# One decoder step on one core: output-projection products in attention's last iterations, weight factors by quarters, more PSUM banks for two output projections

## The chip, the cores and the metric

The kernel runs on one core of one Trainium2 chip. The core has five engines that run side by side, each with its own queue of instructions: TensorE (PE in the rows) multiplies, VectorE (DVE), ScalarE (ACT) and GpSimd (POOL) work on elements, and SyncE (SP) issues most of the transfers between the chip's main memory (HBM) and the on-chip memory (SBUF). TensorE's results go to PSUM, which has eight banks of 128 x 512 float32. The metric is the device time of one execution in microseconds; the kernel before took 2910.5 us, the median of three runs (2903.79 to 2911.71).

## The reference, cut to what matters

One step of a two-layer decoder, for a prompt of 2048 positions and for eight sequences with four new positions each (32 rows, "the sample"). Layer 0 is a gated linear attention, layer 1 an attention over a window of 128 positions and the position itself:

```python
def gla_mixer(h, state0, norm_g, w_in, w_gate2, b_gate, out_norm_g, w_out):
    u = rmsnorm(h, norm_g)
    proj = u @ w_in                       # q, k, v, gate, low-rank gate
    ...
    o, state = gla_recurrence(q, k, v, log_a, state0)
    o = rmsnorm(o, out_norm_g).reshape(bsz, seq_len, BRANCH_WIDTH).astype(h.dtype)
    return (o * jax.nn.silu(gate)) @ w_out, state

def swa_out(o, gate, w_out):
    bsz, seq_len = o.shape[:2]
    return (o.reshape(bsz, seq_len, BRANCH_WIDTH) * jax.nn.silu(gate)) @ w_out

        if layer < N_A_LAYERS:
            ...
            hp, hs = hp + dp, hs + ds
            k_p, v_p = shared_kv(hp, kv_norm, w_k, w_v, k_norm, pos_p)
        else:
            q_p, g_p = swa_query(hp, b_norm[j], b_w_in[j], b_q_norm[j], pos_p)
            hp = hp + swa_out(swa_banded(q_p, k_p, v_p, b_sinks[j]), g_p, b_w_out[j])
            q_s, g_s = swa_query(hs, b_norm[j], b_w_in[j], b_q_norm[j], pos_s)
            hs = hs + swa_out(attend(q_s, k_s, v_s, pos_s, kpos_s, b_sinks[j]), g_s, b_w_out[j])
```

The model width is 1024, the branch width 2048; layer 1 has 32 heads of 64 in 4 groups that share keys and values.

## The kernel before

The prompt is cut into 16 chunks of 128 positions. Each factor of a large product is held as two half-precision parts, high and low, and a product is three passes (high times high, high times low, low times high).

Layer 0 goes through 4 heads x 4 blocks of 4 chunks (h, j). Beside its work stand "preparation steps": they load layer 1's weights, combine and split them on VectorE, GpSimd and ScalarE, and write them to HBM (`wfd`, 7 factors wf0 to wf6) or keep them. `PR` says how many of them (`some(PR[j])`) are woven into each chunk of the block j; what remains is dealt out to the output projection of layer 0, seven to each of its chunks.

Layer 0's output projection (`a_out`, lines 1049 to 1080) takes one chunk after another, each in two halves of 512 columns with 48 products each. `load` fetches the four operands of a chunk with transposing DMAs (tiles sg or v) one chunk ahead, `fin` fetches the input (tile X), adds it to the product on VectorE (line 1064, tiles E and st), stores the sum to `hd`, and normalises the chunk after its second half. Both halves put their product in one of two PSUM banks named pj.

Layer 1's attention (from line 1661) runs 67 iterations. Iteration n projects chunk n % 16 of the group n // 16 (queries, gates, and keys and values in group 0), takes the scores of the chunk two iterations back, and the values of the chunk three back. These three lists are merged by the string ORDER: f is a piece of the projection (the "fill"), A one of four pairs of score heads, B one of two value steps. TensorE's instructions are held in exactly this order (`pin`, line 91). A value step (products kv <- rmask,sth and kv <- rmask,pst of the trace, where rmask holds V) needs the probabilities transposed, which two DMAs on SP's queue do (tiles sth and pst, line 1279); a score pair goes over VectorE (row maxima, line 1268), ScalarE (exponential) and both (split, tile v, line 198) to that queue. At the end of an iteration one step of the sample's attention (`boundary`) is taken: 9 steps of norms and caches, and twice the three steps att (scores, tile ssm), att_2 (transposes and values) and att_3 (product with the gate).

The last three iterations (n = 64, 65, 66) have no chunk left to project. They are filled with products of layer 1's output projection. That one takes 2 chunks at a time (a "pair") and does a 2 x 2 block product with 7 products instead of 8 (`Pair`, PRODS): each is 24 matrix products (0, 1 and 6 on raw operands; 2 to 5 on sums of operands). `load` fetches raw operands with transposing DMAs from `ogd2` (oge in the trace), `sums` forms the others on VectorE and ScalarE (lines 1569 to 1595, among the tiles Sh, wraw, X, ogT, qe, ke), and `fin` adds a finished product to the result (line 1601). The weight factors come from wfd, four DMAs each, all four in one go (`wform`, `wform_big`, tiles W and uT). Six products of pair 0 fill the three iterations; after them the pairs follow one another, each woven with the loads and the sums of the next. The sample's own projection (`out_sample`, with `sproj_steps`) runs in two halves after the pairs 3 and 5, on the banks pj.

Of the kernel before, what the change touches and what calls it, by code (L numbers as in the profile page):

```python
# [56 lines left out]
PR = (2, 4, 2, 0)  # L57
# [17 lines left out]
def _body(tc, nc, cp, sb, ps, dr, i, o):  # L75
# [555 lines left out]
    def sproj_steps(tiles, nk, act_hi_lo, kts=None):  # L631
# [4 lines left out]
        def one(x, w):  # L636
            if x % 8 == 0:
                n = min(8, len(tiles) - x)
                box.append(PT("pj", [P, 512], bufs=2)[:, : n * 2 * SMP].rearrange("p (x z t) -> p x z t", z=2, t=SMP))
# [410 lines left out]
    def a_out(c):  # L1050
# [28 lines left out]
        for half, w in enumerate((wo, wo1)):  # L1079
            st, box = proj_steps(lambda: PT("pj", [P, 512], bufs=2), lambda k, a: ot[k // 8 * 2 + a][:, k % 8, :], w, 16)  # L1080
            out.append(st + [lambda half=half, box=box: fin(half, box[0])])
        return load, out

    def out_sample(tiles, half, finish_s, kts=None, sc=OSC):
        st, total = sproj_steps(tiles, len(kts or range(16)), lambda: ogTs[0], kts)
# [435 lines left out]
    def wform_big(n, parts=1):  # L1521
        t = T("uT", [P, 8, 2, 512], F16, 4)
        for x in range(parts):
            ks = slice(x * 8 // parts, (x + 1) * 8 // parts)
            nc.sync.dma_start(t[:, ks], wfd[n][:, ks])
        wf[n] = lambda k, hl, s=ALL: t[:, k, hl, s]

    def wform(n):
        ts = []
        for x in range(4):  # L1530
            t = T("W", [P, 2, 2, 512], F16, NW)
            nc.sync.dma_start(t, wfd[n][:, 2 * x : 2 * x + 2])
            ts.append(t)
        wf[n] = lambda k, hl, s=ALL: ts[k // 2][:, k % 2, hl, s]
# [4 lines left out]
    TEMP = ("wraw", "Sh", "wraw", "Sh", "wraw", "bt", "bt", "og")  # L1539
# [7 lines left out]
    class Pair:  # L1547
# [3 lines left out]
        def load(self, x):  # L1551

            first = (("og", "lvm"), ("qT", "kT"), ("bt", "bt"), ("S", "sg"))[x]
            ts = [T(tag, [P, 8, P], F16, BUFS.get(tag, 2)) if self.p == 0 else ring("raw", RAW, [P, 8, P], F16) for tag in first]
            for hl in range(2):
                nc.sync.dma_start(ts[hl], ogd2[2 * self.p + x // 2][:, hl, x % 2], transpose=True)
            self.r[x] = ts
            if x != 2:
                self.l[{0: 0, 1: 1, 3: 6}[x]] = ts

        def sums(self):
# [4 lines left out]
            def whole(x, z):  # L1566
                t = ring("temp", TEMP, [P, 512], F32)
# [4 lines left out]
            def put(n, z, t):  # L1572
                if z == 0:
                    self.l[n] = [ring("form", FORM, [P, 8, P], F16) for _ in range(2)]
# [21 lines left out]

            return [lambda f=f, z=z: f(z) for f in (one, two, three, four) for z in range(2)]
# [220 lines left out]
```

## Time and profile before

| what | value |
|---|---|
| median of 3 runs | 2910.5 us (2903.79 to 2911.71) |
| the profiled execution | 2902.2 us |
| its span in the profile | 2900.4 us |
| TensorE busy | 2740.0 us, 94% |
| VectorE busy | 1854.8 us, 64% |
| ScalarE busy | 1440.1 us, 50% |
| GpSimd busy | 1059.9 us, 37% |

The span is what the profile covers from the first to the last instruction; the execution's own time is 1.8 us more. The engines overlap, so the shares do not add up to 100%. The profile also gives the granted clock of TensorE, 1.00 being 2.4 GHz and 0.50 being 1.2 GHz, and DMA's share, the mean busy share of 16 DMA engines (it can exceed 1.00 in a short stretch, since transfers overlap). A timeline row reads: start, duration, engine, line, operation, result <- operands, count, and in brackets the idle time before it and what ended it. In rows of TensorE the line is that of a helper (L101), and tiles tell the place. Tile names are reused: X is a query operand in attention, a formed operand in a pair and an input in a_out.

### The profile page before, as it was taken

How to read it: one execution, taken by the hardware profiler on the slowest of the kernel's cores; microseconds unless marked ns; L12 is line 12 of the kernel's file. 1: busy time of each engine (PE TensorE's matmuls, PEld its weight loads, DVE VectorE, ACT ScalarE, POOL GpSimd, SP SyncE). 2: the span in 40 equal slices, each digit the busy share in tenths (PEclk: the TensorE clock that was granted, in tenths of full speed). 3: DMA queues.
4: the chain of work that ended last, by engine and by line, in shares of the span. 5: the costliest groups of instructions: out<-in, count | busy, mean ns of one | idle time of the engine just before them, and what ended most of it. 6: DMA issues, size and time to landing. Idle time of an engine off the chain costs nothing.

```text
span 2900.4 us, 51645 instructions
## 1 busy us (share of the span) xinstructions
PE 2740.0 (94%) x19070; PEld 1385.9 (48%) x19070; DVE 1854.8 (64%) x3815; ACT 1440.1 (50%) x3385; POOL 1059.9 (37%) x1463
## 2 busy tenths in 40 slices
PE   6899999999999999997999999999999999978999
PEld 4445444444454444444444555555555555534444
DVE  5766787677768775346213665677767767756553
ACT  6655655465546554434212555566666666631110
POOL 2241233222322221136104676666566557520000
PEclk9999999999999999998999999999999999989999
DMA  8351334124312533799765565867867788887542
GB/s 212 85 123 44 88 120 149 38 80 151 118 37 89 169 100 95 175 234 284 180 161 145 109 128 118 201 116 131 174 112 133 164 157 159 159 194 161 108 103 70
DMA packets 765782, 389.68 MB, mean 134 GB/s; under 512 B 620752, under 2 KB 690328, under 8 KB 765496
## 3 DMA queue, kind: packets, MB, share of 16 engines
q1 hardware_dynamic: 752568, 350.65, 53.8%
q0 software_dynamic: 10880, 35.66, 3.4%
q8 instruction: 149, 2.44, 0.4%
q14 instruction: 105, 0.86, 0.1%
q10 hardware_dynamic: 2080, 0.07, 0.0%
HBM read 138.90 MB, written 107.54 MB: 85 GB/s over the span
## 4 chain that ended last, share of the span: by engine, by line
PE 38%; DVE 8%; DMA 7%; ACT 6%; issue 4%; POOL 4%; SPq 1%; DVEq 0%; POOLq 0%; ACTq 0%
PE pj L101 24%; PE tr L101 8%; PE o L101 4%; ACT o L1273 2%; PE kv L101 2%; ACT v L197 1%; DVE v L198 1%; DVE o L1268 1%; DMA pst<-v 1%; DMA sg<-oge 1%; DMA sth<-v 1%; DVE lev L1268 1%; DMA X<-qe 1%; DMA kT<-in_b_w_out_dram 1%; ACT lev L1273 1%
## 5 line engine op out<-in xcount | busy, mean ns | idle before, releaser
L101 PE MATMUL pj<-W,uT 128*128 128x512 f16 x5064 | 1193.2, 381 | 8.4 <-DVE sg L478 2.6
L101 PEld LDWEIGHTS <-uT 128*128 128x128 f16 x6880 | 643.0, 98 | 713.9 <-issue 44.5
L101 PE MATMUL tr<-W,uT 128*128 128x512 f16 x1536 | 365.5, 379 | 0.0
L186 POOL TENSOR_SCALAR rs_m<-ss 128x1 f32<-128x1 f32 (+3 forms) x190 | 45.2, 238 | 738.2 <-ACT og L611 255.7
L101 PEld LDWEIGHTS <-X 128*128 128x128 f16 x2752 | 185.2, 98 | 169.6 <-issue 30.2
L1273 ACT ACTIVATE o<-o,mx 128x256 f32<-128x256 f32 (+1 forms) x384 | 168.6, 439 | 177.9 <-DVE mx L1268 170.2
L101 PE MATMUL pj<-uT,W 128*128 128x512 f16 (+1 forms) x912 | 188.3, 357 | 26.9 <-DMA uT<-ogT 24.2
L1268 DVE CUSTOM_DVE_ANT_0 o<-o,madd,nsink 128x256 f32<-128x256 f32 (+1 forms) x384 | 184.1, 479 | 42.0 <-PE o L101 37.0
L198 DVE SCALAR_TENSOR_TENSOR v<-o,v 128x512 f16<-128x512 f32 (+1 forms) x192 | 129.0, 672 | 111.4 <-ACT v L197 94.9
L187 POOL TENSOR_TENSOR rs_r<-rs_m,mhalf 128x1 f32<-128x1 f32 (+2 forms) x186 | 185.1, 995 | 14.4
L101 PEld LDWEIGHTS <-W 128*128 128x128 f16 x2448 | 130.1, 99 | 113.7 <-issue 19.4
L101 PE MATMUL pj<-W,v 128*128 128x512 f16 x736 | 177.6, 382 | 3.8 <-DVE E L1064 3.8
L101 PEld LDWEIGHTS <-v 128*128 128x128 f16 x1008 | 98.5, 99 | 130.1 <-issue 16.4
L101 PE MATMUL pj<-W,sg 128*128 128x512 f16 x592 | 146.6, 381 | 1.2 <-DVE E L1064 1.2
L195 POOL TENSOR_TENSOR ogT<-og,ogT 128x512 f16<-128x512 f32 x68 | 88.2, 1297 | 158.0 <-ACT ogT L194 153.5
L508 POOL TENSOR_TENSOR E<-bt 128x256 f32<-128x256 f32 x96 | 71.1, 741 | 195.5 <-DVE X L195 112.2
L101 PEld LDWEIGHTS <-sth 128*128 128x128 f16 x2080 | 109.8, 98 | 51.1 <-DMA sth<-v 9.7
L101 PE MATMUL o<-gl,X 128*128 128x256 f16 (+1 forms) x768 | 113.2, 270 | 15.9 <-DMA X<-qe 6.9
L101 PEld LDWEIGHTS <-sg 128*128 128x128 f16 x800 | 78.2, 98 | 97.9 <-issue 6.8
L1273 ACT ACTIVATE lev<-lev,mx 128x256 f32<-128x256 f32 (+1 forms) x128 | 56.5, 442 | 121.2 <-DVE mx L1268 119.1
L197 ACT ACTIVATE v<-o 128x512 f16<-128x512 f32 (+1 forms) x192 | 111.2, 579 | 6.9 <-DMA sth<-v 3.3
L101 PE MATMUL kv<-rmask,sth 128*128 128x64 f16 x1984 | 104.7, 193 | 7.3 <-DMA sth<-v 7.3
(444 smaller groups left out, 5008.6 us busy)
## 6 DMA issues: line engine op xcount, KB each, us to landing
pre<-pst POOLq DMA_DIRECT2D x72, 256.0 KB, 3.5
W<-pre SPq DMA_DIRECT2D x36, 512.0 KB
ogd<-ogT SPq DMA_DIRECT2D x68, 256.0 KB
wraw<-in_a_w_in_dram SPq DMA_DIRECT2D x64, 256.0 KB
wraw<-in_b_w_in_dram SPq DMA_DIRECT2D x64, 256.0 KB
oge<-ogT SPq DMA_DIRECT2D x64, 256.0 KB
wraw<-in_a_w_out_dram SPq DMA_DIRECT2D x32, 256.0 KB
X<-in_x_prompt_dram SPq DMA_DIRECT2D x32, 256.0 KB
```

The costliest lines, as they stand in the source:

```text
L101: return order(nc.tensor.matmul(*a, **k))
L186: pool.tensor_scalar(m[:n, :k], ss, a, b, ALU.mult, ALU.add)
L187: pool.tensor_tensor(r[:n, :k], m[:n, :k], mhalf[:n, :k], ALU.pow)
L195: eng.tensor_tensor(lo, src, hi, ALU.subtract)
L197: act(hi, src, AF.Copy, scale=sc)
L198: dve.scalar_tensor_tensor(lo, src, sc, hi, ALU.mult, ALU.subtract)
L508: pool.tensor_tensor(Ev[:, :, 0, :], ref, btv[:, :, 0, :], ALU.subtract)
L1268: dve.tensor_tensor_reduce(pm[:, z], pm[:, z], madd.rearrange("p a b -> p (a b)")[:, (2 - nk) * P :], -0.125, nsink[:, g * GRP + h : g * G ...
L1273: act(pm[:, z], pm[:, z], AF.Exp, scale=-1.0, bias=nm_[:, h : h + 1], accum_out=bx["sum"][:, h : h + 1])
```

## The change

- Layer 0: `PR` goes from (2, 4, 2, 0) to (1, 4, 2, 0), so nine of its 72 preparation steps there are left to the output projection.
- Layer 0's output projection: half 1 of each chunk takes one of two banks o instead of one of two banks pj.
- The sample's output projections of both layers: half 0 takes the bank lev, half 1 the bank kv, instead of pj.
- Last three attention iterations: they hold products 0 and 1 of pair 0; products 0 and 1 of pair 1; half 0 of the sample's output and product 2 of pair 0. The operands of these products 0 and 1 are fetched at the end of iteration 56 into one tile uT. Pair 0's sums are made in the iterations 65 and 66, one step after another; its other raw operands are loaded in iteration 64 (a list `trickle`, one entry at each third f).
- Weight factors are fetched one quarter per call; those of the last iterations go through `trickle` too.
- The sample's attention steps of the last group are taken twice in each iteration from n = 52 on (at the seventh f, and at the end).
- The tile names of the sums change, and the next pair's loads and sums are woven in another order; half 1 of the sample's output stays after pair 5.

```diff
...
-PR = (2, 4, 2, 0)
+PR = (1, 4, 2, 0)
...
-    def sproj_steps(tiles, nk, act_hi_lo, kts=None):
+    def sproj_steps(tiles, nk, act_hi_lo, kts=None, bank=("pj", 2)):
...
-                box.append(PT("pj", [P, 512], bufs=2)[:, : n * 2 * SMP].rearrange("p (x z t) -> p x z t", z=2, t=SMP))
+                box.append(PT(bank[0], [P, 512], bufs=bank[1])[:, : n * 2 * SMP].rearrange("p (x z t) -> p x z t", z=2, t=SMP))
...
-            st, box = proj_steps(lambda: PT("pj", [P, 512], bufs=2), lambda k, a: ot[k // 8 * 2 + a][:, k % 8, :], w, 16)
+            st, box = proj_steps(lambda half=half: PT(("pj", "o")[half], [P, 512], bufs=2), lambda k, a: ot[k // 8 * 2 + a][:, k % 8, :], w, 16)
...
-        st, total = sproj_steps(tiles, len(kts or range(16)), lambda: ogTs[0], kts)
+        st, total = sproj_steps(tiles, len(kts or range(16)), lambda: ogTs[0], kts, (("lev", "kv")[half], 1))
...
+    def wform_big(n, x, box={}):
+        if x == 0:
+            t = box[n] = T("uT", [P, 8, 2, 512], F16, 4)
+            wf[n] = lambda k, hl, s=ALL: t[:, k, hl, s]
+        ks = slice(2 * x, 2 * x + 2)
+        nc.sync.dma_start(box[n][:, ks], wfd[n][:, ks])
+    def wform(n, x, ts={}):
+        t = ts[n, x] = T("W", [P, 2, 2, 512], F16, NW)
+        nc.sync.dma_start(t, wfd[n][:, 2 * x : 2 * x + 2])
+        wf[n] = lambda k, hl, s=ALL: ts[n, k // 2][:, k % 2, hl, s]
+    quarters = lambda f, n: [lambda x=x: f(n, x) for x in range(4)]
...
         def load(self, x):
-            first = (("og", "lvm"), ("qT", "kT"), ("bt", "bt"), ("S", "sg"))[x]
+            first = (("og", "lvm"), ("qT", "kT"), ("bt", "bt"), ("S", "qe"))[x]
             ts = [T(tag, [P, 8, P], F16, BUFS.get(tag, 2)) if self.p == 0 else ring("raw", RAW, [P, 8, P], F16) for tag in first]
+            self.fetch(x, ts)
+            self.r[x] = ts
+            if x != 2:
+                self.l.setdefault({0: 0, 1: 1, 3: 6}[x], ts)
+        def fetch(self, x, ts):
             for hl in range(2):
                 nc.sync.dma_start(ts[hl], ogd2[2 * self.p + x // 2][:, hl, x % 2], transpose=True)
-            self.r[x] = ts
-            if x != 2:
-                self.l[{0: 0, 1: 1, 3: 6}[x]] = ts
...
+                if self.p == 0:
+                    tag = ("E", "wraw", "wraw", "wraw")[x]
+                    t = T(tag, [P, 512], F32, BUFS.get(tag, 2))
+                else:
+                    t = ring("temp", TEMP, [P, 512], F32)
...
-                    self.l[n] = [ring("form", FORM, [P, 8, P], F16) for _ in range(2)]
+                    own = {2: ("ke", "ke"), 3: ("qe", "X"), 4: ("X", "st"), 5: ("sg", "sg")}[n]
+                    self.l[n] = [T(tag, [P, 8, P], F16, BUFS.get(tag, 2)) if self.p == 0 else ring("form", FORM, [P, 8, P], F16) for tag in own]
...
+            if self.p == 0:
+                return [lambda f=f, z=z: f(z) for z in range(2) for f in (one, two, three, four)]
             return [lambda f=f, z=z: f(z) for f in (one, two, three, four) for z in range(2)]
...
+    trickle, summing = [], []
+    def s_out(half):
+        cols = [slice(z * P, (z + 1) * P) for z in range(4)]
+        right = [k + 2 for k in UP]
+        fs, kts = ((0, 2, 5), UP + UP + right) if half else ((0, 3), UP + right)
+        return out_sample([lambda k, hl, z=z: wf[fs[k // 8]](k % 8, hl, z) for z in cols], half, b_finish_s, kts, OSCB)
...
-            x = 2 * (n - TOT)
-            fill = pairs[0].steps(x) + pairs[0].steps(x + 1)
+            fill = (pairs[0].steps(0) + pairs[0].steps(1), pairs[1].steps(0) + pairs[1].steps(1), s_out(0) + pairs[0].steps(2))[n - TOT]
...
                 upto = len(fill) * seen // nf
                 run(fill[done:upto])
                 done = upto
+                if trickle and seen % 3 == 0:
+                    trickle.pop(0)()
+                if boundary and seen == 7 and n > TOT - NCH + 3:
+                    boundary.pop(0)()
+                if summing and seen % 6 == 3:
+                    summing.pop(0)()
             elif lists[x]:
                 lists[x].pop(0)()
...
-        if n in (TOT - 8, TOT - 5, TOT - 3):
-            wform_big((0, 2, 1)[(TOT - 8, TOT - 5, TOT - 3).index(n)], 4)
+        if n == TOT - 8:
+            t_ = T("uT", [P, 8, 8, P], F16, 4)
+            for x in range(4):
+                pr = pairs[x // 2]
+                pr.l[x % 2] = [t_[:, 2 * x], t_[:, 2 * x + 1]]
+                pr.fetch(x % 2, pr.l[x % 2])
+        if n in (TOT - 6, TOT - 3):
+            run(quarters(wform_big, {TOT - 6: 0, TOT - 3: 2}[n]))
         if n == TOT - 4:
-            wform(3)
-        if n == TOT - 2:
-            pairs[0].load(0)
+            run(quarters(wform, 3))
         if n == TOT - 1:
-            for x in (1, 3, 2):
-                pairs[0].load(x)
+            trickle += [lambda x=x: pairs[0].load(x) for x in (3, 2, 0, 1)] + quarters(wform_big, 1)
         if n == TOT:
-            wform_big(4, 4)
-            run(pairs[0].sums())
+            trickle += quarters(wform, 4) + quarters(wform, 5)
+            summing += pairs[0].sums()
         if n == TOT + 1:
-            wform(5)
-            pairs[1].load(0)
-            pairs[1].load(1)
-        if n == TOT + 2:
-            wform(6)
-            pairs[1].load(3)
-            pairs[1].load(2)
+            trickle += quarters(wform_big, 6)
         if boundary:
             boundary.pop(0)()
...
+    run(trickle + summing)
     for p_ in range(NCH // 2):
         more = []
         if p_ + 1 < NCH // 2:
             nxt = pairs[p_ + 1]
-            if p_ > 0:
-                more += [lambda x=x, nxt=nxt: nxt.load(x) for x in (0, 1, 3, 2)]
-            more += nxt.sums()
-        weave([f for n in range(0 if p_ else 6, 7) for f in pairs[p_].steps(n)], more)
-        if p_ in (3, 5):
-            cols = [slice(z * P, (z + 1) * P) for z in range(4)]
-            right = [k + 2 for k in UP]
-            fs, kts = ((0, 3), UP + right) if p_ == 3 else ((0, 2, 5), UP + UP + right)
-            run(out_sample([lambda k, hl, z=z, fs=fs: wf[fs[k // 8]](k % 8, hl, z) for z in cols], p_ // 5, b_finish_s, kts, OSCB))
+            ld, sm = [lambda x=x, nxt=nxt: nxt.load(x) for x in (2, 3, 0, 1)], nxt.sums()
+            more = ld[:2] + sm[:2] + ld[2:3] + sm[2:6]
+        weave([f for n in range((3, 2, 0)[min(p_, 2)], 7) for f in pairs[p_].steps(n)], more)
+        if more:
+            run(ld[3:] + sm[6:])
+        if p_ == 5:
+            run(s_out(1))
```

The first place is TensorE in the second of the last three iterations, around the last pair of scores (o <- gl,X; gl holds keys). Before:

```order
L101 LDWEIGHTS sg_30681
L101 MATMUL pj_31410<-W_31329,sg_30681 128x512
L101 LDWEIGHTS X_30667
L101 MATMUL o_30997<-gl_15589,X_30667 128x256
L101 LDWEIGHTS X_30930
L101 MATMUL o_31008<-uT_29803,X_30930 128x512
L101 LDWEIGHTS ogT_30931
L101 MATMUL o_31008<-uT_29803,ogT_30931 128x512
```

And in the changed kernel:

```order
L101 LDWEIGHTS uT_29222
L101 MATMUL pj_30920<-W_30209,uT_29222 128x512
L101 LDWEIGHTS X_30805
L101 MATMUL o_31018<-gl_15563,X_30805 128x256
L101 MATMUL pj_31029<-uT_29734,uT_29222 128x512
```

After the scores stood a product 2 of pair 0 on formed operands (X, ogT); now stands a product on the early tile uT, with no sum before it.

The second place is SP's queue from the iteration 63 on (line 1279 transposes probabilities; line 1556, now 1563, loads raw operands of a pair; lines 1525 and 1532 fetch weight factors). Before:

```order
L1532 DMA W_31325<-wf_135 128x2048
L1532 DMA W_31327<-wf_135 128x2048
L1525 DMA uT_30920<-wf_133 128x2048
L1556 DMA_TRANSPOSE qT_30676<-oge_113 128x8x128
L1279 DMA_TRANSPOSE sth_30624<-v_30594 128x8x128
L1279 DMA_TRANSPOSE pst_30626<-v_30595 128x8x128
L629 DMA oge_125<-ogT_30656 512x1x256
L1230 DMA_TRANSPOSE X_30667<-qe_30664 128x8x128
L1556 DMA_TRANSPOSE kT_30677<-oge_113 128x8x128
L1556 DMA_TRANSPOSE S_30680<-oge_114 128x8x128
L1556 DMA_TRANSPOSE sg_30681<-oge_114 128x8x128
```

And in the changed kernel:

```order
L1532 DMA W_31161<-wf_134 128x2048
L1532 DMA W_31216<-wf_134 128x2048
L1527 DMA uT_30925<-wf_130 128x2048 x2
L1563 DMA_TRANSPOSE bt_30847<-oge_114 128x8x128
L1279 DMA_TRANSPOSE sth_30762<-v_30732 128x8x128
L1279 DMA_TRANSPOSE pst_30764<-v_30733 128x8x128
L629 DMA oge_125<-ogT_30794 512x1x256
L1230 DMA_TRANSPOSE X_30805<-qe_30802 128x8x128
L1563 DMA_TRANSPOSE S_30834<-oge_114 128x8x128
L1563 DMA_TRANSPOSE qe_30835<-oge_114 128x8x128
L1563 DMA_TRANSPOSE qT_30916<-oge_113 128x8x128
L1279 DMA_TRANSPOSE sth_30906<-v_30816 128x8x128
```

The loads of qT and kT, which stood around the second pair of transposes, are now behind bt, S and qe, which pair 0's sums need first; one more weight fetch stands ahead.

The third place is VectorE at the first sums of pair 0 (line 1569, now 1577). Before:

```order
L1609 TENSOR_TENSOR E_30914<-E_30914,st_30829 128x512
L198 SCALAR_TENSOR_TENSOR v_30744<-o_30810,v_30743 128x512
L1569 TENSOR_TENSOR Sh_30927<-bt_30684,bt_30685 128x512
L1268 ISA lev_30842,mx_30741<-lev_30842,madd,nsink 128x256
L1268 ISA mx_30741 128x1
L1268 ISA o_30861,mx_30741<-o_30861,madd,nsink 128x256
L198 SCALAR_TENSOR_TENSOR v_30841<-lev_30842,v_30840 128x512
L1315 SCALAR_TENSOR_TENSOR wraw_30900<-kv_30781,sg_30233 128x512
L1569 TENSOR_TENSOR wraw_30925<-S_30680,sg_30681 128x512
```

And in the changed kernel:

```order
L198 SCALAR_TENSOR_TENSOR v_30932<-o_30953,v_30931 128x512
L1612 SCALAR_TENSOR_TENSOR st_31010<-pj_30920,E_31007 128x512
L1268 ISA o_31018,mx_31014<-o_31018,madd,nsink 128x256
L1268 ISA mx_31014 128x1
L1577 TENSOR_TENSOR wraw_31036<-S_30834,qe_30835 128x512
L1577 TENSOR_TENSOR wraw_31038<-bt_30846,bt_30847 128x512
L1589 TENSOR_TENSOR wraw_31036<-wraw_31036,wraw_31038 128x512
L1594 TENSOR_TENSOR wraw_31038<-E_31098,wraw_31038 128x512
L1595 TENSOR_TENSOR E_31098<-wraw_31036,E_31098 128x512
L195 TENSOR_TENSOR ke_31042<-wraw_31036,ke_31041 128x512
L198 SCALAR_TENSOR_TENSOR v_31017<-o_31018,v_31016 128x512
```

The first sum stood behind the first eviction of pair 0, alone and ahead of two score pairs; now two sums stand between two row maxima of the last score pair, and the formed operands follow at once.

## Rows read from the trace of the kernel before

**Rows 1.** The page: its first line, part 1 (busy time, share and instructions of each engine), and one link of the chain of waits (start, length, engine, tile, line, count).

```profile
span 2900.4 us, 51645 instructions
...
PE 2740.0 (94%) x19070; PEld 1385.9 (48%) x19070; DVE 1854.8 (64%) x3815; ACT 1440.1 (50%) x3385; POOL 1059.9 (37%) x1463
...
2677.09 10.36 PE tr L101 x48
```

**Rows 2.** Windows over the last three attention iterations and the pairs behind them. Columns: stretch, its length, then busy time (instructions) of PE, PEld, DVE, ACT and POOL, the granted clock, DMA's share, GB/s.

```profile
2544.20:2616.20 72.00, 53.59 (x361) 26.01 (x361) 39.87 (x90) 22.86 (x66) 10.74 (x17) 0.88 0.84 182
2616.20:2632.20 16.00, 8.91 (x91) 3.94 (x87) 13.81 (x23) 5.18 (x9) 1.16 (x1) 0.68 1.16 237
2632.20:2735.00 102.80, 101.50 (x507) 46.52 (x505) 67.09 (x110) 16.10 (x28) 0.00 (x0) 1.00 0.55 116
2735.00:2750.00 15.00, 9.33 (x117) 5.16 (x114) 4.77 (x8) 0.28 (x1) 0.00 (x0) 0.77 0.57 144
2750.00:2896.50 146.50, 146.43 (x851) 69.37 (x848) 70.11 (x113) 16.69 (x29) 0.00 (x0) 1.00 0.38 88
```

**Rows 3.** The timeline of TensorE in the same stretches: those of its rows before which it stood idle.

```profile
2549.46 0.23 PE L101 MATMUL kv<-rmask,sth 128*128 128x64 f16 x2 [1.24 <-DMA sth<-v]
...
2550.37 0.20 PE L101 MATMUL kv<-rmask,pst 128*128 128x64 f16 x1 [0.67 <-DMA pst<-v]
...
2556.37 1.03 PE L101 MATMUL pj<-W,qT 128*128 128x512 f16 x2 [3.02 <-DMA qT<-oge]
...
2563.07 0.61 PE L101 MATMUL pj<-W,kT 128*128 128x512 f16 x1 [5.67 <-DMA kT<-oge]
...
2580.83 0.39 PE L101 MATMUL o<-uT,ogT 128*128 128x512 f16 x1 [2.19 <-DVE ogT L195]
...
2588.96 0.60 PE L101 MATMUL o<-gl,X 128*128 128x256 f16 x4 [3.37 <-DVE v L198]
...
2625.78 1.04 PE L101 MATMUL o<-uT,X 128*128 128x512 f16 x2 [6.38 <-ACT X L194]
...
2743.22 1.01 PE L101 MATMUL pj<-uT,v 128*128 128x512 f16 x2 [5.67 <-DVE st L1601]
```

**Rows 4.** Windows over five short stretches after such stops, the last one in layer 0's output projection. Columns as in rows 2.

```profile
2556.00:2566.20 10.20, 4.16 (x11) 1.47 (x12) 0.38 (x1) 0.00 (x0) 0.00 (x0) 0.50 1.13 184
2590.00:2597.00 7.00, 5.69 (x17) 2.07 (x16) 3.26 (x10) 2.65 (x7) 0.00 (x0) 0.51 0.34 65
2620.80:2631.00 10.20, 4.51 (x11) 1.40 (x12) 9.14 (x18) 3.92 (x7) 0.00 (x0) 0.50 1.26 247
2740.30:2747.00 6.70, 3.78 (x9) 1.28 (x9) 1.38 (x2) 0.00 (x0) 0.00 (x0) 0.50 0.89 214
1361.30:1375.00 13.70, 8.20 (x137) 6.47 (x137) 8.74 (x10) 6.50 (x13) 9.19 (x13) 0.50 1.09 244
```

**Rows 5.** The waits of TensorE: what it wanted to write, for whom it waited, total us, times, longest us.

```profile
PE kv L101 <- ACT v L197: 9.7, 4, 3.2
PE pj L101 <- DVE st L1064: 9.0, 2, 8.0
...
PE o L101 <- DVE mxs L1462: 5.6, 5, 2.1
...
PE pj L101 <- DVE E L1064: 5.0, 2, 3.8
...
PE tr L104 <- DVE ssg L657: 2.4, 1, 2.4
```

**Rows 6.** The timeline of SP's queue at the start of the last three iterations (start, us, line, operation, result <- source).

```profile
2539.80 4.44 SPq L1279 DMA_TRANSPOSE sth<-v  x1
2544.34 4.01 SPq L1279 DMA_TRANSPOSE pst<-v  x1
...
2552.06 3.13 SPq L1279 DMA_TRANSPOSE sth<-v  x1
2555.28 1.26 SPq L1279 DMA_TRANSPOSE pst<-v  x1
```

**Rows 7.** The timeline of TensorE, VectorE and GpSimd in the last group, at one attention step of the sample (o <- Sh,sq its scores, ssm its weights, tr <- idf,ssm their transposes, ogT the product written), with a value step and a score pair of the prompt between.

```profile
2327.34 0.31 PE L101 MATMUL o<-Sh,sq 128*32 128x128 f16 x8
...
2330.72 0.30 DVE L1468 TENSOR_SCALAR ssm<-ssm,mxs 128x160 f32<-128x160 f32 x1
...
2332.17 0.22 PE L101 MATMUL kv<-rmask,sth 128*128 128x64 f16 x2
...
2332.87 0.59 PE L101 MATMUL pj<-W,uT 128*128 128x512 f16 x2
2333.30 0.60 PE L101 MATMUL o<-gl,X 128*128 128x256 f16 x4
2333.74 1.46 PE L101 MATMUL pj<-W,uT 128*128 128x512 f16 x6
...
2341.78 0.38 PE L104 MATMUL tr<-idf,ssm 128*128 128x128 f32 x2
...
2345.27 0.80 POOL L195 TENSOR_TENSOR ogT<-spp,ogT 128x128 f16<-128x128 f32 x2
```

**Rows 8.** The timeline of VectorE at the first sum of pair 0.

```profile
2567.94 0.69 DVE L1569 TENSOR_TENSOR Sh<-bt,bt 128x512 f32<-128x512 f16 x1 [11.56 <-DMA bt<-oge]
2568.55 0.49 DVE L1268 CUSTOM_DVE_ANT_0 lev<-lev,madd,nsink 128x256 f32<-128x256 f32 x1
```

## What I predicted before the run

> **What bounds the kernel now.** Start with the page [rows 1]: TensorE works 94% of the span, VectorE 64%, and the long links of the chain of waits are bundles of 48 products of 10.36 us, so 0.2158 us for one 128x512 product. The number of products is the same in both kernels, so the time can only move through what is left besides them: TensorE's idle time, and stretches where its granted clock is half. The window view looks for both in the place that the change rewrites, from the last three attention iterations to the end [rows 2]. There TensorE is idle 18.41 + 7.09 + 1.30 + 5.67 + 0.07 = 32.5 us of 352.3, and nearly all of that lies before 2632 and in 2735 to 2750. The timeline of those stretches names each stop [rows 3]: probabilities' transposes (1.24 + 0.67), the operands qT and kT of pair 0's first product (3.02 + 5.67), formed operands (2.19, 6.38), a softmax weight v (3.37), and the bank pj (5.67). In three of four of these stretches the windows show the granted clock at 0.50, the 1.2 GHz level, and in the fourth at 0.51 [rows 4]: TensorE had stood idle just before, and it was busy 5.69 + 4.16 + 4.51 + 3.78 = 18.1 us at that level, which at the full level would be 9.1 us less. So 41.6 us stand in this part to be won. A second place is layer 0's output projection: 5.0 + 9.0 us of waits for VectorE's eviction of line 1064, 2.4 us for the sample's tile ssg [rows 5], and half clock afterwards, 8.2 us busy, 4.1 us too long [rows 4]. That is 20.5 us.
>
> **The tail, part by part.** *Operands of the first products.* qT and kT are loaded before on SP's queue behind transposes that run slowly: 4.44 and 4.01 us where the next pair has 3.13 and 1.26 [rows 6]. The change loads the raw operands of the first products of pairs 0 and 1 eight iterations before, into one tile. The 3.02 and 5.67 go, and products that need no sums fill the second iteration, so the 2.19 and 6.38 for formed operands go too; the sums of pair 0 get two iterations instead of one. *What is late next.* SP keeps its order, and the value transposes (sth, pst) still stand behind weight fetches, nine at that place against eight. I keep the 1.9 us of rows 3 for the first pair. For the others I count: pst of the second pair ends on SP at 2555.28 + 1.26 = 2556.5, and TensorE starts 2.0 us after such an end (2550.37 less 2544.34 + 4.01) [rows 3, 6], so at 2558.5. Between two value steps of an iteration stand 24 products and three scores of 0.44 us (2333.74 less 2333.30), 6.5 us; from 2551.1, where the first pair is done with its 0.7 us (2332.17 to 2332.87) [rows 7], TensorE would be there at 2557.6: 0.9 us late. The chunk after it comes behind X, S, qe and qT: four of 1.3 us from 2557.3, two of 1.3 us, and 2.0 us, together 2567.1. TensorE asks for it after 0.7 us of values, 24 products and a score, 2564.8: 2.3 us late. The bank lev, on which the sample's output waits until the last scores are read, and VectorE's second half of the sums I put at 3 us, pairs 1 and 2, whose sums come sooner after their loads, at 2 us; an estimate between nothing and the 3.37 of v [rows 3], nearer to that. One stretch at half clock stays, 2 us as in 2556 to 2566 [rows 4]. That leaves 12 of 41.6: **30 us won** (at best 41.6, at worst about 12, the case below). *The sample's output.* Its two halves no longer take a pj bank, so product 0 of the pair after it doesn't wait for the eviction of line 1601: the 5.67 and half of the 3.78 are in that sum. *Weight fetches in quarters.* As many bytes, spread between products; DMA's share there is 0.84 to 1.16 [rows 2], so they neither vanish nor grow. I put the wait of SP for the last write of oge before the early load at 1 us, between 0 and the 5.67 that one late operand costs.
>
> **Layer 0's output projection.** Half 1 goes to the banks "o", so four evictions may be outstanding and not two. Of the 20.5 us gross that would take the waits and the half clock behind them. But VectorE's eviction itself waits: the input tile X for it, and the tiles E and st that the store must have left, come from SP's queue, and the transposes of chunk c+2 are queued there behind the store of chunk c. DMA's share is 1.09 in the window at 1361 to 1375 [rows 4], so what doesn't wait for a bank may wait for an operand. I take **half, 10 us**; the bounds are -20 and +3 (one more stop of about the size of the 2.4 [rows 5]).
>
> **The last group's sample steps.** They run twice per iteration there and end seven iterations sooner. Of the chain of one attention step, scores to normalised weights take 2327.34 to 2331.02, 3.7 us, and from the transposes at 2341.78 to the written product at 2346.07, 4.3 us [rows 7]. Two of these steps now have about 16 products, 3.5 us, between them, and TensorE's order is pinned, so the shortfall of 0.2 and 0.8 us, and the sharing of the bank kv two products after, fall on TensorE in part of some fifteen steps. I take **+3 - 1.5** (an iteration that ended with two sample norms loses one), between 0 and +8, 15 times half a microsecond.
>
> **Weight preparation.** Nine of 72 steps move from layer 0 to the output projection, one each into the first block of a row; their DMAs and POOL work go with them. TensorE waits 9.7 us in four places for v in layer 0 and next to it [rows 5]; one step less can shorten these, and the stage that receives them has a DMA share over 1. **-1**, between -9.7 (all of these waits) and +5 (the whole of the E wait doubled).
>
> **The sum.** -30 + 1 - 10 + 1.5 - 1 = -38.5, rounded to -37 because the pieces of the tail overlap. The profiled execution took 2902.2 us, so 2865; the median of the runs shown, 2910.5, is 8.3 above it, so **2873 us**.
>
> **Rivals.** *The queue heads keep the loss.* Before, VectorE stood 11.56 us in front of the first sum, waiting for the load bt, with the row maxima of the next scores behind it [rows 8]. The change puts sums of pair 0 between scores again: their loads S, qe and bt stand on SP among transposes that took 4 us in a bad moment [rows 6]. If VectorE stops there once more as long, 11.6 us come back, with the 3.4 of v behind it [rows 3] and 3 of half clock: 18, and the total is -19, 2891. For it speaks that the loads' place moved by an iteration only; against it that the sums are taken one by one after 12 to 18 products and z by z. The Trainium skill ("TensorE: Matmul & The Clock Gate", section on the array's architectural detail) says that ScalarE's and VectorE's queues are strictly first in, first out, while TensorE's may pull weight loads ahead; the trace agrees, since the row maximum behind the sum started 0.6 us after it and not in the 11.56 us before [rows 8]. By that rule alone, a late bt costs its whole lateness, and the sum would be -37 + 11.6 = -25, 2885. *The banks don't bind.* Then the waits of line 1064 only change their name to X, sg or v loads, and the moved steps cost 3: -37 + 10 + 3 = -24, 2886. *The doubled sample steps stop the pinned order.* If each of the fifteen waits for its whole chain, because its input is written by POOL or ScalarE behind the prompt's work, it costs up to the 3.5 us that lay between: 15 x 3.5 = 52, and the total is +15, **2926**. It decides from 37 / 15 = 2.5 us a step on; before, the stops for mxs were 2.1 us at the longest [rows 5].
>
> **How the numbers follow.** The forecast has 0.62, the queue heads 0.20, the banks 0.10, the sample steps 0.08. 0.3% of the median is 8.7 us, about what a measurement of this kernel tells from no change. The forecast and most of the second and third case lie under 2901.8: 0.62 + 0.14 + 0.09 = 0.85 faster; the rest of these two, 0.07, is within; 0.08 slower. The range: below, -38 in the tail, -14 in the projection and -4 in layer 0 give 2910.5 - 56 = 2854; above, the second case with the sample steps at +8 and the projection at nothing gives 2891 + 6.5 + 4 (part of the ten), about 2902.
>
> **What would show it.** Right: no stop for qT or kT, and windows with the clock near 1.0 from 2550 to 2640; no stop of 5.67 before product 0 after a sample output; the rows for st and E of line 1064 gone, with less than 10 us of new waits for loads; small stops for sth and pst at the start of the tail. Wrong: a VectorE row of a sum with some 10 us of idle before it (second case); waits of pj or o for X, sg or v in the projection, as long as those that went (third); rows of ssm, skn, mxs or ogTs that wait 2 us and more, many times, in the last group (fourth). The forecast falls if TensorE's busy time at full clock grows, which none of the edits should do.

## The result, and the profile after

The changed kernel takes 2880.05 us in the median of four runs (2877.55 to 2887.28), the kernel before on the same chip 2910.97 (2903.79 to 2911.71): a ratio of 0.9903, interval 0.9879 to 0.9928, or 28 us (21 to 35) less. The forecast was 2873 us, 37 less, with a range of 2854 to 2902: the time lies in the range. The gain is three quarters of the forecast, and the forecast 37 lies just outside the interval of 21 to 35. The profiled executions are 2902.2 and 2877.55 us, 24.7 apart. The runs of the kernel before that accompany the experiments spread from 2895.7 to 2915.9, so one profile alone does not tell a few microseconds.

First the page of the changed kernel, to be read beside [rows 1]:

```profile
span 2875.8 us, 51606 instructions
...
PE 2735.2 (95%) x19070; PEld 1386.7 (48%) x19070; DVE 1850.9 (64%) x3815; ACT 1441.6 (50%) x3385; POOL 1062.2 (37%) x1463
```

As many products as before. Where did the time go? Four stages answer: layer 0 up to the second half of its first output chunk; then its output projection and, behind it, the first iterations of attention; attention from there up to iteration 64; and the rest, the tail. The windows of the kernel before (columns as in [rows 2]):

```profile
0.00:1175.59 1175.59, 1101.05 (x6966) 531.45 (x6967) 842.52 (x1516) 678.44 (x1266) 306.48 (x465) 0.98 0.38 107
1175.59:1652.88 477.29, 458.82 (x2635) 217.37 (x2634) 189.79 (x336) 152.14 (x353) 164.36 (x239) 0.98 0.78 185
1652.88:2544.61 891.73, 860.83 (x7568) 486.47 (x7567) 626.14 (x1622) 548.82 (x1637) 577.53 (x745) 1.00 0.73 147
2544.61:2896.43 351.82, 319.34 (x1906) 150.63 (x1903) 195.62 (x342) 60.70 (x132) 11.49 (x16) 0.95 0.57 124
```

And of the changed kernel:

```profile
0.00:1164.22 1164.22, 1099.55 (x6967) 531.65 (x6968) 835.39 (x1507) 672.99 (x1257) 301.82 (x456) 0.98 0.37 104
1164.22:1642.65 478.43, 454.78 (x2636) 215.83 (x2635) 193.65 (x345) 158.88 (x362) 171.40 (x248) 0.98 0.80 195
1642.65:2541.77 899.12, 867.15 (x7628) 489.36 (x7627) 627.83 (x1633) 550.29 (x1642) 576.86 (x745) 0.99 0.73 145
2541.77:2871.77 330.00, 313.77 (x1846) 149.89 (x1843) 193.31 (x332) 59.39 (x127) 12.15 (x16) 0.98 0.64 141
```

The differences of the second column are -11.4, +1.1, +7.4 and -21.8. The forecast had -1, -10, +1.5 and -29, together -38.5; these two profiles have -24.7. Two of the terms are ten off, in opposite directions. The products of the last two stages also have to be read with care: 60 of them, of the sample's last attention step, moved from the tail (x1906, now x1846) to the stage before it (x7568, now x7628). They are small, some 3 us of TensorE's time together, which belong to neither the gain of the one nor the loss of the other.

**Layer 0.** Its idle time, length less busy time, went from 74.5 to 64.7 us. TensorE's waits for v, 9.7 us in [rows 5], are 5.3:

```profile
PE kv L101 <- ACT v L197: 5.3, 4, 1.9
```

**The tail.** The idle time went from 32.5 to 16.2 us. The stops that are left, in TensorE's timeline of the changed kernel (to be held against [rows 3]):

```profile
2548.89 0.23 PE L101 MATMUL kv<-rmask,sth 128*128 128x64 f16 x2 [3.51 <-DMA sth<-v]
2549.76 0.20 PE L101 MATMUL kv<-rmask,pst 128*128 128x64 f16 x1 [0.64 <-DMA pst<-v]
...
2567.09 0.23 PE L101 MATMUL kv<-rmask,sth 128*128 128x64 f16 x2 [1.24 <-DMA sth<-v]
...
2581.34 0.78 PE L101 MATMUL lev<-ogTs,uT 128*128 128x64 f16 x16 [2.90 <-DVE v L198]
...
2624.31 0.61 PE L101 MATMUL tr<-uT,ogT 128*128 128x512 f16 x1 [4.90 <-DVE ogT L195]
```

The stops for qT (3.02) and kT (5.67), for pair 0's formed operands (2.19, 6.38) and for the bank pj (5.67) are gone. The first one, for sth, has grown from 1.24 to 3.51, and 4.90 for a formed operand of pair 1 is new. The 2.90 before the sample's output is the wait for the bank lev that the forecast had put, with something else, at 3 us. The first sum of pair 0, before which VectorE stood 11.56 us [rows 8], now waits 1.21:

```profile
2565.01 0.69 DVE L1577 TENSOR_TENSOR wraw<-S,qe 128x512 f32<-128x512 f16 x1 [1.21 <-DMA qe<-oge]
```

Half clock is left in three stretches, in which TensorE is busy 11.7 us; before it was 18.1 [rows 4]:

```profile
2550.68:2554.09 3.41, 3.41 (x12) 1.52 (x11) 1.52 (x5) 0.00 (x0) 0.00 (x0) 0.50 1.00 362
2581.40:2584.81 3.41, 3.41 (x89) 3.41 (x89) 3.41 (x7) 1.66 (x5) 2.17 (x3) 0.50 1.09 328
2622.36:2629.19 6.83, 4.88 (x12) 1.75 (x13) 6.83 (x13) 0.03 (x1) 0.00 (x0) 0.50 1.04 179
```

SP's queue shows what the first stop and the last wait for: the transposes before 2548, behind five weight fetches, and those of pair 1, behind the copies of the caches (compare the 1.26 of pst in [rows 6]). The first two took 3.51 and 4.95 us, together as long as the 4.44 and 4.01 before [rows 6]; measured against them, TensorE now begins iteration 64 2.3 us sooner.

```profile
2537.64 1.50 SPq L1532 DMA_DIRECT2D W<-wf  x3
2539.24 3.51 SPq L1279 DMA_TRANSPOSE sth<-v  x1
2542.84 4.95 SPq L1279 DMA_TRANSPOSE pst<-v  x1
...
2605.75 0.81 SPq L108 DMA_DIRECT2D out_cks_dram<-in_cache_swa_k_dram  x1
2606.62 0.71 SPq L108 DMA_DIRECT2D out_cvs_dram<-in_cache_swa_v_dram  x1
2607.44 3.21 SPq L1563 DMA_TRANSPOSE sth<-oge  x1
2610.75 7.59 SPq L1563 DMA_TRANSPOSE pst<-oge  x1
```

**Layer 0's output projection.** All waits for line 1064 [rows 5] are gone, and TensorE reaches the second half of the sample's output, after chunk 7, 28 us sooner than before; 11.4 of them it brings along from layer 0. Before:

```profile
1364.38 0.80 PE L101 MATMUL pj<-ogTs,uT 128*128 128x64 f16 x16 [7.96 <-DVE st L1064]
```

In the changed kernel it stops a little further on. The timeline of TensorE and of ScalarE:

```profile
1332.66 3.65 PE L101 MATMUL lev<-ogTs,W 128*128 128x64 f16 x128
1336.14 0.60 PE L101 MATMUL kv<-ogTs,uT 128*128 128x64 f16 x16
...
1360.12 1.03 PE L104 MATMUL tr<-idf,ssg 128*32 128x128 f32 x4 [18.91 <-DVE ssg L657]
...
1351.10 0.63 ACT L197 ACTIVATE Sh<-qT 128x512 f16<-128x512 f32 x1 [2.74 <-DMA qT<-in_b_w_out_dram]
...
1357.18 0.63 ACT L197 ACTIVATE qe<-kT 128x512 f16<-128x512 f32 x1 [2.71 <-DMA kT<-in_b_w_out_dram]
...
1359.05 0.26 ACT L656 ACTIVATE ssg<-lev 128x128 f32<-128x128 f32 x1
```

The sums for ssg were complete at 1336, but ScalarE, which reads them, has preparation steps ahead of them in its queue, and these wait in part for weights from main memory, as the rows of 2.74 and 2.71 us show.

### The profile page after: what moved, and what is told of

Same layout as the page of the kernel before. It is cut to its first block, busy times and chain, and to the rows that moved or that the text cites. A ratio compares the mean times of both kernels' runs of the same rounds, so it can differ in the third digit from the quotient of the medians.

```text
span 2875.8 us, 51606 instructions
## 1 busy us (share of the span) xinstructions
PE 2735.2 (95%) x19070; PEld 1386.7 (48%) x19070; DVE 1850.9 (64%) x3815; ACT 1441.6 (50%) x3385; POOL 1062.2 (37%) x1463
## 5 line engine op out<-in xcount | busy, mean ns | idle before, releaser
L101 PEld LDWEIGHTS <-uT 128*128 128x128 f16 x6976 | 653.3, 98 | 716.1 <-issue 42.0
L101 PE MATMUL kv<-rmask,sth 128*128 128x64 f16 x1984 | 105.7, 193 | 11.4 <-DMA sth<-v 10.5
L101 PE MATMUL kv<-rmask,pst 128*128 128x64 f16 x992 | 100.8, 193 | 7.0 <-DMA pst<-v 7.0
L195 DVE TENSOR_TENSOR X<-E,X 128x512 f16<-128x512 f32 x128 | 95.6, 747 | 13.4 <-ACT X L194 13.1
```

What stands on the lines that cost most here:

```text
L101: return order(nc.tensor.matmul(*a, **k))
L195: eng.tensor_tensor(lo, src, hi, ALU.subtract)
```

## The experiments

Ratios are against the kernel before in the same session, with 95% intervals.

**The three parts, each alone.** First the moved preparation steps:

```diff
-PR = (2, 4, 2, 0)
+PR = (1, 4, 2, 0)
```

> The kernel before with only PR = (1, 4, 2, 0). By the trace of the changed kernel TensorE reaches the first output-projection chunk 11.4 us sooner, so theory A (the nine moved steps are worth that much, since they stood in the first block of each head) expects 2911 - 9 to - 12 = about 2900. Theory B (as predicted, the moved steps are worth 1 us, and the 11.4 us come from something else or from run-to-run spread) expects 2907 to 2913, no difference that can be told.

Measured: 2894.12 us, 0.9966 (0.9952 to 0.9979), some 10 us less: A by the time. The trace agrees: layer 0, 1175.6 us in the kernel before, takes 1159.2 in it. Over all profiles of this case that stage lasts 1173.6 to 1178.1 us with the old PR (five profiles) and 1159.2 to 1164.3 with the new one (eight). The next part is the bank of half 1:

```diff
-            st, box = proj_steps(lambda: PT("pj", [P, 512], bufs=2), lambda k, a: ot[k // 8 * 2 + a][:, k % 8, :], w, 16)
+            st, box = proj_steps(lambda half=half: PT(("pj", "o")[half], [P, 512], bufs=2), lambda k, a: ot[k // 8 * 2 + a][:, k % 8, :], w, 16)
```

> The kernel before with only half 1 of layer 0's output projection on the banks o; the sample's output keeps pj. Theory A (TensorE's lead of 16 to 18 us over the chunks 0 to 7 is handed back at the sample's output, whose eviction stands on ScalarE and VectorE behind the preparation steps, which wait for their own loads) expects a stop of 15 to 25 us before the tile ssg and a time within 4 us of the kernel before, 2907 to 2913. Theory B (as predicted, half of the 20 us is won) expects about 2901.

Measured: 2907.78 us, 1.0013 (0.9999 to 1.0027). A holds: nothing won, and the stop is there, with the sample's output on its old bank:

```profile
1374.87 1.04 PE L104 MATMUL tr<-idf,ssg 128*32 128x128 f32 x4 [20.02 <-DVE ssg L657]
```

The third is the changed kernel with these two put back:

> The changed kernel with PR and the bank of half 1 of layer 0's output projection put back. What is left is the tail, the sample's output banks and the doubled sample steps. Theory A (the trace: tail -20.5, sample steps and what belongs to attention +6) expects -13 to -17, about 2896. Theory B (as predicted: tail -29, sample +1.5) expects -27, 2884.

Measured: 2893.28 us, 0.9959 (0.9944 to 0.9975): -12, just under A's -13 to -17 and far from B's -27. Its tail, from iteration 64 on, is 20.8 us shorter than before, its stretch of attention 12 us longer. Added up, the three give -0.62%, the whole change -0.97%, each known to about 0.25 either way; that the parts help each other is not excluded and not shown.

**The stop before ssg.** The changed kernel with the sample's output in layer 0 moved:

```diff
-        if c == 7:
+        if c == 12:
             for half, w in enumerate((wo, wo1)):
```

> The changed kernel with the sample's layer-0 output taken after chunk 12 instead of after chunk 7. If TensorE's stop of 18.9 us before ssg comes from where that output stands (chunk 7, when the preparation steps hold ScalarE's and VectorE's queues up), theory A expects the stop to shrink to under 8 us and 10 to 18 us to be kept: 2862 to 2870. Theory B (preparation limits the whole stage, so that TensorE's lead is lost at the next place that needs these queues) expects the stop, here or at the end of the projection, and a time of 2876 to 2884 as the changed kernel has.

Measured: 2873.82 us, 0.9893 (0.9872 to 0.9913). The stop is gone; in its place stand waits for the operand loads of the next chunks, in TensorE's waits:

```profile
PE pj L101 <- DMA sg<-ogd: 5.5, 3, 3.0
...
PE pj L101 <- DMA v<-ogd: 4.7, 3, 3.0
```

10.2 us for 18.9: the projection's stage is 7 us shorter (471.4 against 478.4). Both theories were half right. The place made the stop, and behind it lies the next limit, the loads on SP's queue, at a DMA share of 1.03 to 1.09 in these stretches. The total was too close to the changed kernel's, which ran in another session, to tell alone; the next session ran that kernel again, beside this edit together with another one.

**The copies, and both places late.** The changed kernel again:

> The changed kernel as it is, so that the next two can be held against it on the same chip: 0.990 of the kernel before, between 0.988 and 0.993 by its first runs. If the runs of both kernels spread as they did (0.4%), the profile's parts should come out again: about -11 in layer 0, the stop of 15 to 20 us before ssg, about -20 in the tail.

Measured: 2877.73 us, 0.9898 (0.9881 to 0.9915). It came out again, stage by stage within 3.4 us. Then the copies:

```diff
-    for n, (od, ca) in enumerate((("cks", "cache_swa_k"), ("cvs", "cache_swa_v"))):
-        later(o[od][:, : WIN - TS], i[ca][:, TS:])
...
+        if p_ == 3:
+            for n, (od, ca) in enumerate((("cks", "cache_swa_k"), ("cvs", "cache_swa_v"))):
+                later(o[od][:, : WIN - TS], i[ca][:, TS:])
```

> The changed kernel with the two copies of the caches (line 108, main memory to main memory) issued after pair 3 instead of before pair 0. In the changed kernel the transposing loads of pair 1 that follow these copies on SP's queue took 3.2 and 7.6 us instead of 1.25, and TensorE stood 4.9 us before the formed operand ogT. Theory A (the copies slow those loads) expects these loads at 1.2 to 2 us, the stop gone or under 1 us, and 4 to 8 us less than the changed kernel. Theory B (the loads are slow from the weight quarters beside them, or the sums are late on VectorE anyway) expects the stop to stay and no change over 2 us.

Measured: 2880.6 us, 0.9901 (0.9885 to 0.9917), no change. The same loads on SP's queue:

```profile
2600.58 1.37 SPq L1563 DMA_TRANSPOSE sth<-oge  x1
2602.05 1.28 SPq L1563 DMA_TRANSPOSE pst<-oge  x1
```

And the stop on TensorE:

```profile
2617.56 0.61 PE L101 MATMUL tr<-uT,ogT 128*128 128x512 f16 x1 [2.81 <-DVE ogT L195]
```

A's cause is right, since the loads take 1.3 us without the copies; its price is not. The stop only shrinks to 2.8 us, because the sums were nearly as late on VectorE: its wait of 5.2 us for pst is gone, but the operand is ready only 1.5 us sooner, counted from the start of iteration 64. And another of 2.3 us appears at 2685, before a product of a later pair. With both places late:

> The changed kernel with the copies late and the sample's layer-0 output after chunk 12. If the two are independent, the sum of both: 4 to 8 us from the copies and 4 to 8 from the sample's output (whose stop of 18.9 us was replaced by about 10 us of waits for operand loads in the run before), so 8 to 16 us under the changed kernel. If the first of them was spread between chips, only the copies' part.

Measured: 2866.97 us, 0.9865 (0.9847 to 0.9883), 11 us under the changed kernel in the medians of one session; the intervals overlap a little. Against the run with the copies alone late, 2880.6, the only difference is the sample's place, and it is 13.6 us. The projection's stage is 467.3 us against 478.8 in the changed kernel.

**The sample's steps, twice per iteration,** on the kernel before:

```diff
                 done = upto
+                if boundary and seen == 7 and n > TOT - NCH + 3:
+                    boundary.pop(0)()
```

> The kernel before with only the sample's attention steps of the last group taken twice per iteration. Theory A (the trace of the changed kernel, where the stretch from the output projection's end to iteration 64 is some 6 us worse with the moved steps taken out) expects +3 to +7 in that stretch, part of it given back because the last three iterations hold no sample steps: 2906 to 2912 against 2906. Theory B (the predicted +1.5) expects no difference that can be told, and no stop of 2 us at ssm, mxs, skn or ogTs beyond those there before.

Measured: 2902.62 us, 0.9984 (0.997 to 0.9998): slightly faster, if anything, so a net cost, as A has it, is not seen. In the profile attention up to iteration 64 is 8.4 us longer and the tail 4.4 shorter, but only a part of this stands where the edit acts. The doubled steps begin in iteration 52. The windows from the value step of iteration 51, just ahead of them, to iteration 64, first of the kernel before, then of this run:

```profile
2359.60:2544.61 185.01, 179.27 (x1636) 103.34 (x1635) 135.66 (x346) 118.52 (x357) 117.49 (x148) 1.00 0.85 167
2363.04:2552.19 189.15, 183.06 (x1695) 105.28 (x1694) 136.21 (x356) 119.56 (x364) 116.83 (x149) 0.99 0.78 160
```

That is 4.1 us, some 3 of them the 60 products that moved out of the tail; the idle time grew by 0.4. The other 4.3 us lie ahead of iteration 51, where the program is the same in both kernels, at a granted clock of 0.99 against 1.00. The lower clock is no sign of this edit: the runs with PR alone and with the sample's banks alone, which do not have it, fall to half clock in the last group too (at 2303; at 2313 and 2442), and the run with the copies alone late, which has it, does not. TensorE's waits for mxs are 6.0 us in five places, 2.5 at the longest, hardly more than in [rows 5]. This is nearest to B: the doubled steps cost about 1 us by the profile, and by the timed runs they gain between nothing and 9; how they could gain is open.

**The sample's banks alone,** the two outputs of the kernel before on lev and kv:

```diff
-        st, total = sproj_steps(tiles, len(kts or range(16)), lambda: ogTs[0], kts)
+        st, total = sproj_steps(tiles, len(kts or range(16)), lambda: ogTs[0], kts, (("lev", "kv")[half], 1))
```

> The kernel before with only the sample's two outputs on the banks lev and kv (layer 0 and layer 1, at their old places). Theory A (as predicted for the tail: the 5.67 us stop before product 0 of pair 4 goes with half of the 3.78 us behind it, some 7.5 us) expects the row pj<-uT,v gone from the waits and 2899 to 2903 where before is 2907. Theory B (the product waits for its operands or for the next eviction anyway) expects a stop of 3 us or more in its place.

Measured: 2901.48 us, 0.9983 (0.9967 to 0.9999), 5 us less, where A expected 4 to 8: A by the time, with an interval that nearly reaches no change. In the profile the tail is 3.8 us shorter, half of the 7.5 expected. The 5.67 for pj [rows 3] is gone, but TensorE now stands just ahead of that place:

```profile
2743.35 1.03 PE L104 MATMUL tr<-idf,ssg 128*32 128x128 f32 x4 [4.54 <-DVE ssg L657]
```

So B, as a stop. VectorE shows why: in both kernels it stands there before the next results that it has to add, waiting for a load (tile E, from hd), and both the eviction of pj before and ssg here are behind that in its queue. First the kernel before, then this run:

```profile
2738.17 0.69 DVE L1609 TENSOR_TENSOR E<-E,E 128x512 f32<-128x512 f32 x1 [3.50 <-DMA E<-hd]
...
2738.07 0.69 DVE L1609 TENSOR_TENSOR E<-E,E 128x512 f32<-128x512 f32 x1 [3.33 <-DMA E<-hd]
```

In the changed kernel half 0 stands in an iteration, and VectorE has no such wait at that moment: the sums end at 2586.1, ssg is ready at 2587.8, and TensorE does not stop for it. That the place does this, and not the bank, is read from the traces; no run moved half 0 alone.

**Two edits to the version with both places late,** and that version again. No preparation in the first block of a head:

```diff
-PR = (1, 4, 2, 0)
+PR = (0, 4, 2, 0)
```

> The version with both late places and PR = (0, 4, 2, 0): no preparation steps in the first block of a head, nine more in the output projection. Theory A (the head boundaries still wait 5 us in all for v, since ScalarE and VectorE work through these steps there) expects 3 to 6 us less in layer 0. Theory B (the projection, whose operand loads already wait at a DMA share above 1, takes the nine steps worse) expects that gain to come back there, no change or up to +4 over the run without this edit.

Measured: 2883.31 us, 0.9911 (0.9894 to 0.9929), 10 us more than without the edit in that session (2873.19, the last run below). Neither theory: layer 0 itself got 5.8 us longer (1170.1 against 1164.3), where A expected 3 to 6 less, and the waits for v are back, which were 5.3 us in the changed kernel:

```profile
PE kv L101 <- ACT v L197: 9.1, 5, 3.0
```

The list of steps is consumed in order, so PR also decides which step stands at a head's boundary. "Fewer is better" is refuted; which step it is was not tried. The last edit keeps the fetches of the factors 4 and 5 where the program issues them:

```diff
-        nc.sync.dma_start(t, wfd[n][:, 2 * x : 2 * x + 2])
+        d = nc.sync.dma_start(t, wfd[n][:, 2 * x : 2 * x + 2])
+        if n > 3:
+            tc.keep_in_program_order(d)
```

> The version with both late places, and the quarter fetches of the factors 4 and 5 kept on SP's queue where the program issues them; the scheduler had put six of the eight ahead of the transposes of the first of the last three iterations. Theory A (these fetches slow the transposes to 3.5 and 5.0 us) expects both at 1.2 to 1.4 us, the first stop of 2.4 to 3.5 us before kv<-rmask,sth under 0.5 us, those around the second and third value step smaller, and 3 to 6 us less than the run without this edit. Theory B (the transposes are slow from the load of main memory by other transfers) expects the stop to stay, and the later fetches to add one before the products 4 and 5.

> The version with both late places again, as the run that the two before are held against on the same chip: 0.9865 of the kernel before, between 0.985 and 0.988.

Measured: 2864.61 us, 0.9851 (0.983 to 0.9873), against 2873.19, 0.9884 (0.9864 to 0.9903), for the version without it. SP's queue without the edit:

```profile
2533.40 1.64 SPq L1532 DMA_DIRECT2D W<-wf  x3
2535.13 3.73 SPq L1279 DMA_TRANSPOSE sth<-v  x1
2538.96 4.87 SPq L1279 DMA_TRANSPOSE pst<-v  x1
```

With it, where the transposes follow no weight fetch:

```profile
2527.75 0.66 SPq L1621 DMA_DIRECT2D E<-hd  x1
2529.41 1.24 SPq L1279 DMA_TRANSPOSE sth<-v  x1
2530.75 1.28 SPq L1279 DMA_TRANSPOSE pst<-v  x1
```

TensorE's stop there, 0.58 us for pst and, for sth, the one of this row without the edit, is absent with it:

```profile
2544.92 0.29 PE L101 MATMUL kv<-rmask,sth 128*128 128x64 f16 x2 [3.76 <-DMA sth<-v]
```

A new stop of 2.06 us, for ssg, takes a part of this back, and the tail is 3.4 us shorter (327.4 against 330.9). A holds: the fetches slow the transposes. Of the 8.6 us between the two medians only these 3.4 can be laid to the edit; in the same two profiles the projection's stage, which it does not touch, differs by 3.6. The change had spread these fetches in the program, but the scheduler had put five of the eight, not six as expected, ahead of that iteration's first transposes and two more ahead of the second pair; these two are the rows of W in the second place of the section on the change. This version is the fastest one: 0.9851 against 0.9898 and 0.9903 for the changed kernel, though its interval's upper end, 0.9873, is close to theirs. The third session's version came out at 0.9884 where 0.985 to 0.988 were expected, so sessions differ by some 0.2%, and against 0.9865 for the same version in the second session the gain of the last edit is 0.14%.

## Why the prediction came out so

- **The tail, -29, came out at -21.8,** of which some 3 us are products that only moved out of it. The mechanism was right: the stops for qT, kT and the formed operands of pair 0 went, the clock of the stretch rose from 0.95 to 0.98, and the second case, VectorE standing before the first sum, did not happen (1.21 us). The term that was mis-sized is "that leaves 12 of 41.6": 16.2 us of idle time were left, and 11.7 us busy at half clock, of which half, 5.9, is lost, so 22. Three entries make up the difference. The first pair of transposes, put at 1.9 us as before, cost 4.2, because TensorE came to it sooner and the transposes, behind a burst of weight fetches, took as long as before; the run with the fetches kept in order shows that the burst is what makes them long. Pairs 1 and 2, put at 2 us, cost 6.1, 4.9 of them in one stop of pair 1, part of it from the copies of the caches, which the forecast left out. And half clock, put at one stretch and 2 us, came in three.
- **"Its two halves no longer take a pj bank",** -7.5 in that sum, named half of the cause. On the banks alone the tail won 3.8 us, and the stop moved to ssg, 4.54 us, since VectorE's wait for the load E stayed. In the changed kernel it is gone with the move of half 0 into the iteration.
- **Layer 0's output projection, -10, came out at +1.1.** The step that failed is "half, 10 us". The banks did remove the waits of line 1064, but the time was lost again at the next product that waits for ScalarE and VectorE: the sample's output after chunk 7, 18.9 us, and the banks alone came out at 1.0013. This is the third case, the banks that don't bind, with another wait than those I named; with the sample's output out of the way, the loads v and sg that I had named came, 10.2 us. My upper bound of +3 held.
- **Weight preparation, -1, came out at -11.4,** outside the bound of -9.7. The bound took the waits for v as all that these steps could cost. They went by 4.4 us (9.7 to 5.3); all idle time of the stage went by 9.9, the rest in smaller waits for other tiles, and the busy time by 1.5. Half clock had no part in it: TensorE was busy at that level for 30.6 us of the stage before and 32.3 after (22.5 in the run with these steps alone, which makes some 4 us there). How a step holds up those other tiles was not traced.
- **The sample's steps, +1.5,** came out at +7.4 in the stage, of which some 3 us are moved products. The fourth case, 52 us, is excluded by the run that had them alone, and that run leaves about 1 us or less for them.
- **The total.** Two errors of ten, -10.4 in the weight preparation and +11.1 in the projection, nearly cancel. That the forecast time came within 7 us is luck in this part; the miss that is left is mainly the tail's.

## What to carry to other kernels

In this kernel more banks let the matrix engine run ahead only as far as the next result that the slower engines had to hand back in their queue's order (18.9 us lost there for 14 us of waits won): find that place before counting the waits as won, and move it to where those engines are not behind. A transfer spread out in the program is spread only if the scheduler leaves it there, so read the issue order of the queue. And a stop can have two prices, its length and the half clock after it [rows 4]; the second belongs in the bounds. Last, when work moves between stages, count the products of each stage before reading its time as a gain or a loss.

## What the runs showed of the hardware

Transposing loads of one shape took 1.24 to 1.37 us on SP's queue in the runs where the weight fetches or the copies ahead of them had been taken away. They took 3.5 to 5.0 us behind a burst of five weight fetches, and 3.2 to 7.6 behind the copies from main memory to main memory: up to six times as long.
